# Half of each Q cast moved to ScalarE, three of eight scalings instead of two on GpSimd, last stores split: strided attention on one Trainium2 core

## Chip, cores and metric

The kernel runs on one core of a Trainium2 chip. The metric is the device time of one execution in microseconds (us). Every run has a state; all runs used here for comparison are in the fast state, and where a run fell in the slow one the text says so. The profile's engines are PE (TensorE), DVE (VectorE), ACT (ScalarE), POOL (GpSimd) and SPq (the sequencer of SyncE, which issues all transfers).

## The reference

```python
batch, heads, seq, dim = 8, 12, 1024, 64        # Q, K, V float32; stride 64
attend_positions = np.arange(0, seq, stride)    # the same 16 keys for every query
for i in range(seq):
    scores = einsum('bhqd,bhkd->bhqk', Q[:, :, i:i+1], K[:, :, attend_positions]) / sqrt(dim)
    weights = softmax(scores)
    result[:, :, i] = einsum('bhqk,bhkd->bhqd', weights, V[:, :, attend_positions])
```

All of Q (25.2 MB) is read, the result (25.2 MB) is written, and of K and V only every 64th row is needed. There is little arithmetic for each byte.

## The kernel before

The 96 heads are worked in 24 groups of four. A group's 1 MB block of Q is loaded, cast to bf16 on GpSimd, transposed on VectorE, multiplied with keys placed block-wise (`scores`), put through exp on ScalarE, multiplied with values (`outputs`, in three parts of 3, 2 and 3 token blocks), and divided by the sums of the weights, which come out of the same matmul.

```python
    def cast(g):
        qb[g] = qb_pool.tile([P, 32 * D], BF16, name="qb", tag="qb")
        nc.gpsimd.tensor_copy(out=qb[g], in_=qn[g])
    # ...
    def outputs(g, c):            # c = 0, 1, 2: 3, 2, 3 token blocks
        # ... n matmuls into ps, reciprocal r on VectorE
        if n == 3:
            nc.vector.tensor_tensor(out=to, in0=o, in1=by, op=ALU.mult)
        else:
            nc.scalar.copy(to, o)
            nc.gpsimd.tensor_tensor(out=to, in0=to, in1=by, op=ALU.mult)
    # ...
    key_rows(0)
    cast(0)
    cast(1)
    keys(0, 0)                    # two copies on ScalarE, two on VectorE
    transpose(0)
    scores(0)
    # ...
    for g in range(NG):           # each engine runs its instructions in this order
        # ahead(g): transpose(g+2), scores(g+1), values(g+2), cast(g+3); outputs(g, 0..2)
        if g % 2 == 1:
            for a in range(2):
                store(g // 2, a)                      # 1 MB
                if g - 1 + a + QBUFS < NG:            # QBUFS = 10 blocks of Q in SBUF
                    load(g - 1 + a + QBUFS)
```

All loads and stores go through one queue in the order in which they are written: K, block 0, V, blocks 1 to 9, then store, load, store, load for each pair of groups, and stores alone once all 24 blocks are loaded.

The softmax here doesn't subtract the row's maximum and nothing guards it: scores larger than these inputs give would overflow.

## Time and profile before

| What | Value |
|---|---|
| time, three runs | 129.98, 130.06, 130.66 us |
| span of the profiled run | 128.2 us |
| VectorE, GpSimd, TensorE, ScalarE busy | 75, 70, 54, 45% |
| transfer queue busy | 96.1% |

These groups of instructions (busy us in all, mean ns of one, idle time before them) are the ones that the change touches:

```profile
L199 POOL CAST qb<-qn 128x2048 bf16<-128x2048 f32 x24 | 45.3, 1889 | 3.9 <-DMA qn<-in_Q_dram 3.9
L249 DVE TENSOR_TENSOR out_sb<-o_ps,rec 128x768 f32<-128x768 f32 x48 | 46.0, 958 | 1.7
L252 POOL TENSOR_TENSOR out_sb<-out_sb,rec 128x512 f32<-128x512 f32 x24 | 25.0, 1042 | 23.2 <-ACT out_sb L251 23.2
L251 ACT COPY out_sb<-o_ps 128x512 f32<-128x512 f32 x24 | 14.1, 586 | 23.7 <-DVE rec L247 16.6 <-issue 5.5 <-POOL qb L199 1.6
```

The number before the comma is the busy time of the whole group: 46.0 us of VectorE goes into scalings, 45.3 us of GpSimd into casts, while ScalarE copies only 14.1 us. That is the imbalance that the change goes for.

### The profile page before, as it was taken

What the parts mean: (1) busy time and instruction counts of PE and PEld (TensorE: products, weight loads), DVE (VectorE), ACT (ScalarE), POOL (GpSimd) and SP (SyncE); (2) the same over time, 40 slices, a digit from 0 to 9 for tenths busy, and PEclk for the clock granted to TensorE, in tenths of its full rate; (3) what the DMA queues carried; (4) which work ended last, traced back from release to release, by engine and by line L of the source; (5) the groups of instructions that cost most, each with busy time, mean ns of one, the idle gap of its engine ahead of it and who ended that gap; (6) DMA issues with size and microseconds to landing.
All of it is one profiled execution on the core that took longest, in us unless ns stands there. A gap on an engine that the chain in (4) does not pass through costs nothing.

```text
span 128.2 us, 1125 instructions
## 1 busy us (share of the span) xinstructions
PE 69.1 (54%) x292; PEld 30.9 (24%) x292; DVE 95.6 (75%) x167; ACT 57.7 (45%) x96; POOL 90.2 (70%) x89
## 2 busy tenths in 40 slices
PE   0004267886763796348674664696436973465100
PEld 0001022342321343114331332333212431132000
DVE  6947557677988778898789888888889788987300
ACT  4110603638592448785264644535364255462100
POOL 8952489966888576897969888897889878533300
PEclk9999999999999559996579998559995589997555
DMA  2999989999998999999989999999999999989593
GB/s 64 363 325 465 470 358 470 409 419 389 430 417 368 476 394 430 440 384 432 488 363 440 440 419 435 424 404 470 419 404 435 419 424 424 424 353 440 251 430 164
DMA packets 6373, 51.18 MB, mean 399 GB/s; under 512 B 3872, under 2 KB 3872, under 8 KB 3872
## 3 DMA queue, kind: packets, MB, share of 16 engines
q1 hardware_dynamic: 6368, 51.12, 96.1%
q8 instruction: 2, 0.03, 0.1%
q14 instruction: 3, 0.02, 0.0%
HBM read 25.95 MB, written 25.17 MB: 399 GB/s over the span
## 4 chain that ended last, share of the span: by engine, by line
DVE 54%; PE 17%; issue 9%; DMA 8%; POOL 4%; SPq 1%; ACT 0%; POOLq 0%
DVE out_sb L249 32%; DVE qt L203 14%; PE o_ps L239 13%; DMA qn<-in_Q_dram 8%; DVE rec L247 7%; PE sc L210 4%; POOL out_sb L252 2%; POOL qb L199 1%; POOL v L191 1%; DVE v_rep L184 1%; SPq L35 1%; ACT out_sb L251 0%; SPq L100 0%; DVE k_r L159 0%; SPq L98 0%
## 5 line engine op out<-in xcount | busy, mean ns | idle before, releaser
L239 PE MATMUL o_ps<-v,w 128*128 128x260 bf16 x192 | 41.0, 340 | 34.0 <-DVE out_sb L249 32.5
L221 ACT ACTIVATE w<-sc 64x512 bf16<-64x512 f32 x48 | 35.5, 739 | 31.7 <-PE sc L210 31.0
L199 POOL CAST qb<-qn 128x2048 bf16<-128x2048 f32 x24 | 45.3, 1889 | 3.9 <-DMA qn<-in_Q_dram 3.9
L249 DVE TENSOR_TENSOR out_sb<-o_ps,rec 128x768 f32<-128x768 f32 x48 | 46.0, 958 | 1.7
L210 PE MATMUL sc<-qt,k_t 128*128 128x512 bf16 x96 | 34.7, 497 | 13.6 <-DVE qt L203 12.1
L252 POOL TENSOR_TENSOR out_sb<-out_sb,rec 128x512 f32<-128x512 f32 x24 | 25.0, 1042 | 23.2 <-ACT out_sb L251 23.2
L239 PEld LDWEIGHTS <-w 128*128 128x128 bf16 x192 | 19.2, 116 | 62.3 <-DVE out_sb L249 46.2
L203 DVE STREAM_TRANSPOSE qt<-qb 128x1024 int32<-128x1024 int32 x24 | 29.6, 1232 | 5.2 <-POOL qb L199 5.2
L247 DVE RECIPROCAL rec<-o_ps 128x12 f32<-128x12 f32 (+1 forms) x72 | 15.3, 213 | 15.9 <-PE o_ps L239 15.9
L251 ACT COPY out_sb<-o_ps 128x512 f32<-128x512 f32 x24 | 14.1, 586 | 23.7 <-DVE rec L247 16.6
L191 POOL TENSOR_TENSOR v<-mask,v_rep 128x256 bf16<-128x256 bf16 x24 | 16.0, 668 | 2.3 <-DVE v_rep L184 2.3
L210 PEld LDWEIGHTS <-k_t 128*128 128x128 bf16 x96 | 11.1, 116 | 24.9 <-issue 12.0
L169 ACT COPY k_t<-k_r 32x128 bf16<-32x128 bf16 x20 | 5.9, 295 | 1.7 <-DVE k_r L159 1.5
L129 POOL MEMSET k_t<- 128x4608 bf16 x1 | 3.9, 3935 | 0.0
L180 PE MATMUL vp<-v_bf,perm_v 128*128 128x384 bf16 x4 | 1.5, 413 | 2.4 <-DVE v_rep L184 2.4
L158 ACT CAST k_bf<-k_raw 128x256 bf16<-128x256 f32 x3 | 1.2, 405 | 3.5 <-DMA k_raw<-in_K_dram 3.4
L139 DVE TENSOR_SCALAR s_sel<-col,slot_f 128x4 bf16<-128x4 int16 x1 | 2.5, 2547 | 0.1
L184 DVE CAST v_rep<-vp 128x384 bf16<-128x384 f32 x4 | 2.1, 544 | 0.6 <-PE vp L180 0.6
L123 DVE MEMSET k_t<- 128x1152 uint32 x1 | 1.0, 1018 | 1.0 <-PEq L321 1.0
L158 ACT ACT_TABLE_LOAD x1 | 1.3, 1283 | 0.7 <-PEq L321 0.7
L127 DVE MEMSET w<- 128x512 uint32 x3 | 1.5, 485 | 0.2
L118 POOL COPY perm_v<-identity 128x32 bf16<-128x32 bf16 x8 | 1.2, 209 | 0.0
(16 smaller groups left out, 4.8 us busy)
## 6 DMA issues: line engine op xcount, KB each, us to landing
qn<-in_Q_dram SPq DMA_DIRECT2D x24, 1024.0 KB, 13.6
out_dram<-out_sb SPq DMA_DIRECT2D x24, 1024.0 KB, 11.2
k_raw<-in_K_dram SPq DMA_DIRECT2D x1, 384.0 KB, 4.7
v_raw<-in_V_dram SPq DMA_DIRECT2D x1, 384.0 KB, 7.8
```

The lines of the kernel that those rows point to most:

```text
L129: nc.gpsimd.memset(k_t[:, 8:NG], 0.0)
L169: op(k_t[dst : dst + 32, 8 * m + c : 8 * m + 8 : 2, :, col : col + NK], k_r[src : src + 32, 4 * m : 4 * m + 4].rearrange("p n (a k f) -> p ...
L191: nc.gpsimd.tensor_tensor(out=vb[g][:, 0 : 4 * D].rearrange("p (s d) -> p s d", s=4), in0=mask, in1=v_rep[:, g // 2, g % 2].unsqueeze(1).t ...
L199: nc.gpsimd.tensor_copy(out=qb[g], in_=qn[g])
L203: nc.vector.transpose(qt[g].bitcast(I32), qb[g].bitcast(I32))
L210: nc.tensor.matmul(sc, lhsT=k_t[:, g, f, NK * (1 - e) : NK * (1 - e) + P], rhs=_ap_with(q, [q.ap[0], [D, 8], [16 * D, 2], [2, 32]], extra_ ...
L221: nc.scalar.activation(out=_ap_with(wa, [wa.ap[0], [P, 8], [4, 32], [2, 2]], extra_offset=a), in_=sc[64 * a : 64 * a + 64].rearrange("p (t ...
L239: nc.tensor.matmul(ps[:, i, 0 : 4 * D + 4], lhsT=wt[g][:, i0 + i], rhs=vb[g], start=True, stop=True,)
L247: nc.vector.reciprocal(r, ps[:, 0:n, 4 * D : 4 * D + 4])
L249: nc.vector.tensor_tensor(out=to, in0=o, in1=by, op=ALU.mult)
L251: nc.scalar.copy(to, o)
L252: nc.gpsimd.tensor_tensor(out=to, in0=to, in1=by, op=ALU.mult)
```

## The change

ScalarE takes half of every cast. GpSimd scales three token blocks of eight instead of two (with ScalarE copying them out of PSUM first), VectorE five instead of six. The last two groups are stored each as soon as it is done.

```diff
     def cast(g):
         qb[g] = qb_pool.tile([P, 32 * D], BF16, name="qb", tag="qb")
-        nc.gpsimd.tensor_copy(out=qb[g], in_=qn[g])
+        half = 16 * D
+        nc.gpsimd.tensor_copy(out=qb[g][:, 0:half], in_=qn[g][:, 0:half])
+        nc.scalar.copy(qb[g][:, half:], qn[g][:, half:])
...
-        if n == 3:
+        if c < 2:
             nc.vector.tensor_tensor(out=to, in0=o, in1=by, op=ALU.mult)
...
-    def store(n, a):
-        o = out_2[n][a : P : 2]
+    def store(g, groups, a):
+        o = out_sb[g][a : P : 2]
...
-        if g % 2 == 1:
+        if g >= NG - 2:
+            for a in range(2):
+                store(g, 1, a)
+        elif g % 2 == 1:
             for a in range(2):
-                store(g // 2, a)
+                store(g - 1, 2, a)
                 if g - 1 + a + QBUFS < NG:
                     load(g - 1 + a + QBUFS)
```

More of the change, by code (lines that the diff above doesn't have):

```diff
@@ L259, in store @@
             _ap_with(
-                out, [[16 * D, 64], [2 * SD, 4], [1, 16 * D]],
-                2 * n * HG * SD + a * SD,
+                out, [[16 * D, 64], [2 * SD, 2 * groups], [1, 16 * D]],
+                g * HG * SD + a * SD,
             ),
-            _ap_with(o, [o.ap[0], [1, 1], [1, 64 * D]]),
+            _ap_with(o, [o.ap[0], [1, 1], [1, 32 * groups * D]]),
         )
```

## The prediction

> **What bounds the kernel now.** I began with the page's parts 1 and 2. No engine is full (VectorE 75%, GpSimd 70%, TensorE 54%), but the row of the DMA engines stands at 8 or 9 tenths from the second slice to the last few:
>
> ```profile
> DMA  2999989999998999999989999999999999989593
> ...
> q1 hardware_dynamic: 6368, 51.12, 96.1%
> ```
>
> Each digit is a fortieth of the span, 3.2 us. The queue that SyncE fills is busy 96.1% of 128.2 us, 123.2 us, for 51.12 MB. So the kernel is bound by transfers, and only the 5 us in which they stand still can be won. The second view, busy time in chosen stretches, shows where those are (the last two columns are the share of the DMA engines and GB/s; a share can pass 1 where packets overlap):
>
> ```profile
> 2.00:30.00 28.00, 13.02 (x39) 5.25 (x39) 19.15 (x37) 8.96 (x17) 20.69 (x19) 1.00 1.02 400
> ...
> 30.00:114.00 84.00, 53.24 (x240) 24.65 (x240) 70.56 (x121) 45.12 (x77) 65.96 (x58) 0.84 1.00 423
> 114.00:115.00 1.00, 0.40 (x2) 0.11 (x2) 0.89 (x2) 0.98 (x2) 0.02 (x1) 1.00 0.47 197
> 115.00:120.00 5.00, 2.46 (x11) 0.84 (x11) 3.60 (x9) 1.40 (x3) 1.97 (x2) 0.69 1.01 426
> 120.00:121.00 1.00, 0.00 (x0) 0.00 (x0) 0.41 (x1) 0.00 (x0) 0.11 (x1) 0.50 0.09 33
> 121.00:122.00 1.00, 0.00 (x0) 0.00 (x0) 0.00 (x0) 0.00 (x0) 0.00 (x0) 0.50 0.62 262
> 122.00:125.00 3.00, 0.00 (x0) 0.00 (x0) 0.00 (x0) 0.00 (x0) 0.00 (x0) 0.50 1.04 437
> 125.00:127.00 2.00, 0.00 (x0) 0.00 (x0) 0.00 (x0) 0.00 (x0) 0.00 (x0) 0.50 0.62 262
> ```
>
> From 2 to 114 us there is no hole. Then come three: 0.53 us before the second-last pair of groups is stored, 0.91 + 0.38 = 1.29 us before the last pair, and about 0.8 us at the very end, where some transfers end before others. The chain of waits (54% VectorE, 8% DMA) must be read with this in mind: it follows the last store back through compute, and that compute mattered only after 114 us.
>
> The start comes third, because compute must offer the first store before the first loads run out. Until 30 us the queue moved 374 GB/s x 30.0 us = 11.22 MB; the ten first blocks of Q (10 x 1.049 MB) with K and V (2 x 0.393 MB) are 11.27 MB. So the loads end at about 30.1 us. The timeline has the first store there only just in time:
>
> ```profile
> 7.35 0.60 ACT L169 COPY k_t<-k_r 32x128 bf16<-32x128 bf16 x2 [1.50 <-DVE k_r L159]
> 8.12 1.89 POOL L199 CAST qb<-qn 128x2048 bf16<-128x2048 f32 x1 [1.58 <-DMA qn<-in_Q_dram]
> 11.34 1.86 PE L210 MATMUL sc<-qt,k_t 128*128 128x512 bf16 x4 [11.34 <-DVE qt L203]
> 12.30 1.89 POOL L199 CAST qb<-qn 128x2048 bf16<-128x2048 f32 x1 [2.29 <-DMA qn<-in_Q_dram]
> 28.16 0.64 SPq L35 DMA_DIRECT2D out_dram<-out_sb  x1
> ```
>
> Data of a store moves about 0.9 us after its issue starts (estimate from the last pair: issued 120.47, and 262 of 437 GB/s in 121 to 122 us puts the start near 121.4). Issued at 28.16, the first store is ready at 29.1, one microsecond before the loads run dry.
>
> [...]
>
> **The change part by part.**
>
> *Work for each group of four heads.* VectorE drops one 768-element scaling (0.958 us) and takes one of 512[...]: busy 3.79 (0.64 reciprocals, 1.92 scalings, 1.23 transposition) becomes 3.5 us. GpSimd's cast of 2048 elements, 1.89, is halved to about 0.97; its scaling grows from 512 elements (1.04) to 768, about 1.45 by the slope between its 256-element (0.67) and 512-element products; values stay 0.67: 3.6 becomes 3.1. ScalarE has two exponentials (1.48), a copy grown from 0.59 to about 0.80, and a new half cast[...]: 2.07 becomes 3.3. The load is evened out, and nothing exceeds the old 3.8.
>
> *Pace of compute.* With the full TensorE clock a group takes 4.09 us now (scaling to scaling, 104.86 to 108.95), and VectorE is nearly full in it. Afterwards the loop is VectorE's 3.5 or a two-group loop through ScalarE copy, GpSimd scaling, values, cast and transposition, about 3.7. At the half clock the loop scaling, three matmuls (0.83), four score matmuls (1.9), first output matmuls, reciprocal takes 4.5 now (98.53 to 103.04) and contains nothing that changes. I take 3.95 instead of 4.2 as the mean. But both are under the DMA's need of 2.10 MB / 423 GB/s = 4.96 us per group, so between 30 and 114 us this is worth nothing for the end. It only makes the queue longer.
>
> *The tail.* With a queue that never empties, and with the last two groups stored when each is done (group 22 some 3 us earlier, only 1.05 MB left behind the last scaling), the two holes of 0.53 and 1.29 us go: **-1.8 us**. The uneven end of 0.8 us stays. The last scaling's own route gets longer (copy 0.80, GpSimd 1.45, against 0.96 on VectorE, about +1.3 us), but transfers queued in front cover it.
>
> *The start.* Here the order of instructions matters. ScalarE's half of cast(1) is written before the key copies keys(0,0), which the first scores need. ScalarE runs in order, so those copies (at 7.35 now) wait for Q block 1, which GpSimd receives at 12.30. Half cast to 13.3, two key copies to 13.9, scores(0) 13.9 instead of 11.34, first exponentials 15.8 to 17.4, second value matmul[...] to 17.9. So outputs(0) begin at 17.9 instead of 16.72: +1.2. Then group 0's last scaling is on GpSimd behind a ScalarE copy: copy 21.1 to 21.9, scaling to 23.4, values(2) to 24.1, half cast(3) to 25.1; transpose(3), which VectorE holds in front of group 1's reciprocals, starts at 25.1 instead of 23.14. First reciprocal of group 1 at 26.4 instead of 24.70; from there 4.65 us (two scalings, matmuls, copy, GpSimd scaling) instead of 3.46 to the store. The first store comes at about 31.1 instead of 28.16. Its data then starts at 32.0, the loads ended at 30.1: a hole of **+1.9 us** which no later work gives back, as the queue is full from there on. I followed the next stores the same way (40, 49, 58 us, against 36.93, 47.22, 55.59 now): each arrives before the queue is empty, if sometimes by only a microsecond.
>
> *Sum.* 130.06 - 1.8 + 1.9 = 130.2. The start is an addition of a dozen small terms of which I tended to take the long side, so I put the prediction at 129.9.
>
> **Rivals.** (a) The start isn't delayed as far as the loads' end: if the store comes before 29.2, only the tail counts, 130.06 - 1.8 = 128.3. For it: GpSimd's and ScalarE's halves run side by side, 0.9 us sooner per cast. Against it: the order of cast(1) and the keys is in the code, and the copy plus GpSimd scaling is longer by 1.3 us. (b) Compute is the bound, and relieving VectorE saves 24 x 0.25 = 6 us: 124. The chain of waits speaks for it, the full DMA row from 2 to 114 us against it; the floor of transfers, 51.12 MB at 423 GB/s = 120.9 us plus start, uneven end and close, leaves no room below about 128. (c) ScalarE becomes the bound: with keys (1.2 us) its groups 2, 3, 6, 7 need 4.5 us; if each semaphore wait costs a little more, stores 2 to 4 come late, more holes open early, and the time goes to 131.5 to 132.5. Its idle waits for scores (31.0 us now) say that it has room on average, but its position between PSUM banks and exponentials says that a late copy delays the next group's exponentials.
>
> **Range and chances.** The best case with no early hole is 128.3, the case with a hole of 3 us is 131.3; 128.4 to 131.4 should hold it 8 times in 10. Faster by over 2% needs under 127.46, below the floor of transfers: 0.05. Slower by over 2% needs over 132.66, an early loss of over 4.4 us: 0.05. Within 2%: 0.90.
>
> **What would show it.** Right: the key copies on ScalarE start near 13.3, the first store near 31, DMA rates fall in 30 to 32 us, no hole at 114 or 120, GpSimd casts near 1.0 us, VectorE's 512-element scaling 0.69, all compute done by about 121 while the queue is still long. Wrong: a first store before 29.2 (then 128.3), a hole between 40 and 60 us (rival c), or a queue still empty before the last store, which would mean that the pace of compute had become slower than 4.96 us per group.

## The result, and the profile after

The changed kernel took 131.88 us (median of four runs, 131.69 to 132.59); the kernel before, in the same rounds and the runs that came first, 130.28 us (129.98 to 130.66). Ratios here are the mean time of one kernel's fast runs over the mean of the other's fast runs of the same rounds, so they differ a little from the ratio of the medians. The ratio is 1.013, with an interval of 1.008 to 1.018: slower, though by less than 2%. The measured time lies 0.5 us above the predicted range.

The page of the changed kernel answers the first view of the prediction:

```profile
DMA  3999989997979999999999999999999999999991
...
q1 hardware_dynamic: 6528, 51.12, 96.0%
```

The queue is as busy as before, 96.0%, now of 130.1 us. The end of the row is full, as predicted; the 7s in slices 10 and 12 (from 29 and 36 us) are new. (A share counts a packet whole in the slice in which it starts. By the records of single packets only the first 7 is a standstill; in slice 12 the engines are busy with packets that started before it. A share over 1 can have two reasons: from 5 to 30 us of the kernel before up to 24 packets are on record at once, and the share is 1.02 even with packets cut at the window's edges; from 122 to 125 us, 1.04 becomes 1.01 in this way.) The groups of instructions, by form:

```profile
L201 ACT CAST qb<-qn 128x1024 bf16<-128x1024 f32 x24 | 25.1, 1045 | 7.6 <-DMA qn<-in_Q_dram 7.0
L200 POOL CAST qb<-qn 128x1024 bf16<-128x1024 f32 x24 | 24.9, 1037 | 5.2 <-DMA qn<-in_Q_dram 5.2
...
L254 POOL TENSOR_TENSOR out_sb<-out_sb,rec 128x768 f32<-128x768 f32 x24 | 35.3, 1471 | 29.4 <-ACT out_sb L253 29.4
L253 ACT COPY out_sb<-o_ps 128x768 f32<-128x768 f32 x24 | 19.2, 798 | 14.6 <-DVE rec L249 14.3
L251 DVE TENSOR_TENSOR out_sb<-o_ps,rec 128x512 f32<-128x512 f32 x24 | 16.6, 692 | 0.8
```

The engines do what the change meant them to do: casts on GpSimd fall from 45.3 to 24.9 us, scalings on VectorE from 46.0 to 39.6 (23.0 of 768-element ones and the 16.6 shown). None of this is where the time is. The start of the changed kernel, in its timeline:

```profile
7.71 1.04 ACT L201 CAST qb<-qn 128x1024 bf16<-128x1024 f32 x1 [2.22 <-DMA qn<-in_Q_dram]
...
11.87 1.04 ACT L201 CAST qb<-qn 128x1024 bf16<-128x1024 f32 x1 [3.11 <-DMA qn<-in_Q_dram]
...
12.82 0.60 ACT L169 COPY k_t<-k_r 32x128 bf16<-32x128 bf16 x2
...
13.47 1.89 PE L212 MATMUL sc<-qt,k_t 128*128 128x512 bf16 x4 [13.47 <-ACT k_t L169]
...
30.36 0.63 SPq L35 DMA_DIRECT2D out_dram<-out_sb  x1
```

ScalarE's half of block 1's cast waits for that block until 11.87 us, the key copies come behind it at 12.82, though their source `k_r` is ready at 7.31, and the first scores wait for them until 13.47 us, against 11.34 before. The first store is issued at 30.36 us, against 28.16. What that does to the queue is in the view of chosen stretches (last columns: granted TensorE clock, DMA share, GB/s), first of the changed kernel, then of the kernel before:

```profile
30.00:31.00 1.00, 0.47 (x3) 0.00 (x0) 0.97 (x3) 0.96 (x3) 1.00 (x3) 0.50 0.01 0
31.00:32.00 1.00, 0.28 (x2) 0.22 (x3) 0.96 (x3) 0.98 (x1) 0.94 (x1) 0.50 0.62 262
32.00:38.00 6.00, 5.11 (x18) 2.27 (x17) 4.64 (x9) 5.02 (x9) 3.08 (x3) 0.50 1.04 306
38.00:114.00 76.00, 46.64 (x230) 22.74 (x229) 61.51 (x116) 62.97 (x88) 55.95 (x54) 0.88 1.00 425
114.00:125.00 11.00, 1.69 (x8) 0.50 (x6) 2.23 (x5) 1.45 (x2) 2.94 (x2) 0.54 0.99 417
125.00:127.00 2.00, 0.00 (x0) 0.00 (x0) 0.00 (x0) 0.00 (x0) 0.00 (x0) 0.50 0.90 377
127.00:129.00 2.00, 0.00 (x0) 0.00 (x0) 0.00 (x0) 0.00 (x0) 0.00 (x0) 0.50 0.18 74
```

```profile
32.00:38.00 6.00, 4.34 (x20) 1.90 (x18) 5.45 (x9) 4.55 (x11) 4.99 (x6) 1.00 1.01 399
38.00:114.00 76.00, 47.49 (x216) 22.02 (x216) 63.96 (x111) 39.14 (x63) 60.08 (x52) 0.82 1.00 426
```

Three things are to be seen. First, the queue stands still at 30 us. The view makes it 0.99 + 0.38 = 1.4 us, but it counts each packet whole where it starts. By the records of single packets, those of load 9 end at 30.68 to 31.21 us (mean 30.89) and those of the first store begin at 31.65 to 31.79 (mean 31.70), so an engine stands still for 0.8 us on average. Second, and this was not foreseen, from 32 to 38 us the DMA engines are busy all the time (share 1.04) but move 306 GB/s instead of 399: the packets themselves take longer. By the records of single packets, 16 KB pieces of the first store go from 0.62 to 1.26 us and 32 KB pieces of the load behind it take about 1.75 instead of 1.22. Over all packets from 28 to 40 us this is 1.5 us more for each engine than before (1.9 against 0.4, in the table under x12). Third, the rate between 38 and 114 us is the same in both kernels, 425 and 426 GB/s: the new division of work is worth nothing there. And at the end the share falls over more than two microseconds, 0.90 and then 0.18: some engines end much later than others.

**A second look at the end.** The page counts 16 DMA engines, and the trace records the landing of a transfer in 16 steps (800 for the 50 transfers of the kernel before, 832 for the 52 of the changed one). I take one step for each engine. The trace has the time of each step but not the engine's name, so for every transfer one can work out when the median engine and when the last engine ended. This is my own working from the trace, times in us from the span's start:

```
                           before: median, last     changed: median, last
load 9 (last of the first)     31.1   32.1               31.3   31.7
first store, first half        33.8   34.5               35.4   35.5
load 10                        36.3   37.5               39.0   39.2
load 11                        41.4   42.4               44.0   44.7
store of groups 20 and 21     120.7  121.6              122.6  124.2
last store                    127.0  127.1              127.4  129.1
```

The engines fall out of step early and stay so: in the kernel before, the first and the last of the 16 are 1.0 to 1.4 us apart until 44 us and 2.0 to 2.2 us apart from 51 to 115 us; in the changed one 0.3 to 1.2 and then 2.1 to 2.3. In these two traces they come together by more than 0.3 us only where the queue has run empty: in the changed kernel from 0.57 us at load 9 to 0.26 at the first store, behind the hole at 30 us; in the kernel before they are 2.2 us apart at the landing of 116.65 us, 1.0 behind the hole at 114 us, and 0.2 behind the one at 120 to 122. Across the two holes the landings of the median engine are 3.1 and 3.9 us apart, those of the last engine 2.5 and 3.1, so it is the fast ones that waited. The changed kernel has no hole there, and its engines are 2.3 us apart at the last store.

So the holes at the end of the kernel before were mostly holes of the fast engines. The last steps of its last five transfers fall at 116.65, 119.12, 121.56, 124.70 and 127.14 us. They are 2.4 to 2.5 us apart, as in the stretch before, except for one of 3.14: the slowest engine did not notice the hole at 114 us at all, and lost 0.7 us, not 1.29, in the one at 120 to 122. Between load 11 and the store of groups 20 and 21, the last engine took 79.1 us before and 79.5 after; for what followed it took 5.6 us before (hole included) and 4.9 after. The whole difference of the last column, 2.0 us, is then 2.2 us up to load 11, 0.4 in the middle, and -0.6 at the end (from unrounded times).

### The profile page after: what moved, and what is told of

It reads as the page before. It is cut to its first block, busy times and chain, and to the rows that moved or that the text cites.

```text
span 130.1 us, 1201 instructions
## 1 busy us (share of the span) xinstructions
PE 65.9 (51%) x292; PEld 30.6 (24%) x292; DVE 88.8 (68%) x167; ACT 86.3 (66%) x120; POOL 80.1 (62%) x89
## 3 DMA queue, kind: packets, MB, share of 16 engines
q1 hardware_dynamic: 6528, 51.12, 96.0%
## 4 chain that ended last, share of the span: by engine, by line
DMA 35%; POOL 23%; issue 17%; DVE 5%; ACT 4%; PE 4%; SPq 1%; POOLq 1%; DVEq 0%; ACTq 0%
DMA qn<-in_Q_dram 35%; POOL out_sb L254 9%; POOL qb L200 8%; POOL v L191 5%; DVE out_sb L251 3%; PE sc L212 3%; ACT qb L201 2%; DVE qt L205 1%; POOLq L340 1%; ACT out_sb L253 1%; PE o_ps L241 1%; DVE rec L249 1%; ACT k_t L169 1%; ACT w L223 1%; SPq L35 1%
## 5 line engine op out<-in xcount | busy, mean ns | idle before, releaser
L241 PE MATMUL o_ps<-v,w 128*128 128x260 bf16 x192 | 39.0, 325 | 36.0 <-DVE out_sb L251 31.8
L254 POOL TENSOR_TENSOR out_sb<-out_sb,rec 128x768 f32<-128x768 f32 x24 | 35.3, 1471 | 29.4 <-ACT out_sb L253 29.4
L251 DVE TENSOR_TENSOR out_sb<-o_ps,rec 128x768 f32<-128x768 f32 (+1 forms) x48 | 39.6, 824 | 1.9 <-DVE rec L249 0.3
L212 PE MATMUL sc<-qt,k_t 128*128 128x512 bf16 x96 | 33.2, 481 | 14.0 <-ACT k_t L169 13.5
L201 ACT CAST qb<-qn 128x1024 bf16<-128x1024 f32 x24 | 25.1, 1045 | 7.6 <-DMA qn<-in_Q_dram 7.0
L253 ACT COPY out_sb<-o_ps 128x768 f32<-128x768 f32 x24 | 19.2, 798 | 14.6 <-DVE rec L249 14.3
L200 POOL CAST qb<-qn 128x1024 bf16<-128x1024 f32 x24 | 24.9, 1037 | 5.2 <-DMA qn<-in_Q_dram 5.2
L212 PEld LDWEIGHTS <-k_t 128*128 128x128 bf16 x96 | 10.9, 114 | 24.9 <-ACT k_t L169 13.5
L159 DVE STREAM_TRANSPOSE k_r<-k_bf 128x128 int32<-128x128 int32 x3 | 0.9, 308 | 2.3 <-ACT k_bf L158 2.3
```

The costliest lines, as they stand in the source:

```text
L200: nc.gpsimd.tensor_copy(out=qb[g][:, 0:half], in_=qn[g][:, 0:half])
L201: nc.scalar.copy(qb[g][:, half:], qn[g][:, half:])
L212: nc.tensor.matmul(sc, lhsT=k_t[:, g, f, NK * (1 - e) : NK * (1 - e) + P], rhs=_ap_with(q, [q.ap[0], [D, 8], [16 * D, 2], [2, 32]], extra_ ...
L241: nc.tensor.matmul(ps[:, i, 0 : 4 * D + 4], lhsT=wt[g][:, i0 + i], rhs=vb[g], start=True, stop=True,)
```

## The experiments

My theory after this reading was: (1) the hole before the first store costs its own length, (2) packets behind it are slow, and (3) the end is set by the slowest DMA engine, so filling the holes at the end pays only 0.6 us. The rival was that ScalarE's and GpSimd's new work slows the pace of compute. All kernels gave correct results. The numbers:

| Kernel | median us (lowest to highest) | ratio to before, interval |
|---|---|---|
| changed | 131.88 (131.69 to 132.59) | 1.013, 1.008 to 1.018 |
| x1 stores alone | 129.36 (129.22 to 129.47) | 0.993, 0.988 to 0.998 |
| x2 casts alone, its two fast runs of four | 131.68 (130.85 and 132.51) | 1.011, 1.000 to 1.021 |
| x3 copies and scalings alone | 132.33 (131.61 to 132.55) | 1.015, 1.009 to 1.020 |
| x4 changed, first groups as before | 129.89 (129.48 to 130.28) | 0.997, 0.992 to 1.002 |
| x5 changed, last stores as a pair | 131.71 (131.35 to 132.19) | 1.009, 1.002 to 1.017 |
| x6 changed, keys in front of cast(1) | 130.36 (130.01 to 130.45) | 0.999, 0.993 to 1.005 |
| x7 before, first store made late | 134.48 (133.38 to 135.15) | 1.030, 1.022 to 1.039 |
| x8 changed, loads two places ahead | 129.68 (129.45 to 129.79) | 0.994, 0.988 to 1.000 |
| x9 = x8 and extra loads on 8 engines | 132.33 (131.66 to 132.63) | 1.014, 1.007 to 1.020 |
| x10 changed, 8 engines kept busy | 133.70 (133.52 to 133.90) | 1.025, 1.018 to 1.032 |
| x11 before, stores alone, loads ahead | 129.36 (129.17 to 129.66) | 0.992, 0.987 to 0.997 |
| x12 changed, first two stores together | 131.50 (131.20 to 131.85) | 1.011, 1.003 to 1.019 |

The medians are of four runs each (x2: two, x11: six). The kernel before had medians of 130.08 to 130.29 us beside them, between 129.05 and 131.44 in its fast runs (one of its runs, beside x12, was slow). The batches ran at different times and on different chips, so differences between batches of a few tenths of a us are not to be read.

**x1: the single stores alone.** The kernel before with only the hunks of `store` and of its calls:

```diff
-        if g % 2 == 1:
+        if g >= NG - 2:
+            for a in range(2):
+                store(g, 1, a)
+        elif g % 2 == 1:
```

> Theory (the queue is the bound; the change lost time because the queue ran empty before the first store, its first packets afterwards were slow, and its engines ended unevenly): the stores alone leave the start as before, so the first store at 28.2 us, no hole there, 30 to 40 us at about 410 GB/s or more. At the end the hole of 1.3 us before the last pair goes, the uneven end may grow by up to 1 us: 128.8 to 130.1, best guess 129.3. Rival (the pace of compute, with more waits on ScalarE and GpSimd, is what costs): the stores touch no engine, so the same gain at the end, but no statement on unevenness: 128.7.

It took 129.36 us, 0.9 us less than the 130.25 beside it, and the start was as before (first store at 27.65 us, 433 GB/s from 32 to 38 us). The split of the stores is the good part of the change. The gain is about half of the 1.8 us that the prediction had booked, and near the 0.6 us of the last engine's column.

**x2 and x3: the casts alone, the copies and scalings alone.** x2 is the kernel before with the first of these two hunks, x3 with the second:

```diff
-        nc.gpsimd.tensor_copy(out=qb[g], in_=qn[g])
+        half = 16 * D
+        nc.gpsimd.tensor_copy(out=qb[g][:, 0:half], in_=qn[g][:, 0:half])
+        nc.scalar.copy(qb[g][:, half:], qn[g][:, half:])
...
-        if n == 3:
+        if c < 2:
```

> Theory: the split cast alone delays the first scores (ScalarE's key copies after block 1) to about 13.5 us, but shortens GpSimd's casts; the scaling stays on VectorE for six of eight blocks, so the first store at 28 to 29.3 us, hole at most 0.3 us: 129.8 to 130.6. Rival (ScalarE's longer queue is what costs): ScalarE has 3.1 us per group instead of 2.1, so most of the 1.8 us of loss should show here: 131.5 or more.

> Theory: the copy and scaling of three blocks on ScalarE and GpSimd, with GpSimd's whole casts, put 4.0 us per group on GpSimd and lengthen the route of group 0 and 1: first store at 30 to 31.5 us, a hole of 1 to 2 us at 30 us, slow packets after it (under 350 GB/s in 32 to 38 us); 131.5 to 133.5. Rival (ScalarE): ScalarE has only 2.3 us per group here, so near 130.

x2 is inconclusive: its profile and one more run of four fell in the slow state, and its two fast runs are 130.85 and 132.51 us, both above what the theory expected (129.8 to 130.6). In its profile the first store is at 28.56 us. x3 did what the theory said: first store at 30.09 us, no transfer from 30 to 31 us, 303 GB/s from 32 to 38 us, and 132.33 us, although ScalarE has little more to do in it than before.

**x4: the changed kernel with the first groups as before.**

```diff
     def cast(g):
+        if g < 4:
+            nc.gpsimd.tensor_copy(out=qb[g], in_=qn[g])
+            return
...
-        if c < 2:
+        if c < 2 if g >= 2 else n == 3:
```

> The changed kernel, but blocks 0 to 3 cast whole on GpSimd and groups 0 and 1 scaled as before. Theory: first store at 28.2 to 28.5 us, no hole, no slow stage after it (over 400 GB/s in 30 to 40 us), no hole at 114 and 120 us, uneven end as in the changed kernel (about 1.5 us): 128.3 to 129.5, best guess 128.9, faster than both kernels. Rival (steady pace or ScalarE bound): 20 of 24 groups are as in the changed kernel, so 131 to 132.

129.89 us: the first store at 28.14 us, 396 GB/s from 32 to 38 us, and 2.0 us less than the changed kernel, while the steady pace is the changed one for 20 of 24 groups. So the loss lies in the first groups, and the rival falls. The time is 0.5 us above x1 and 0.4 above my range, and the landings say why: the median engine ended its last store at 124.8 us, the last engine 2.25 us later.

**x5: the last two groups as a pair again.** The changed kernel with `store` and its calls as in the kernel before:

```diff
-        if g >= NG - 2:
-            for a in range(2):
-                store(g, 1, a)
-        elif g % 2 == 1:
+        if g % 2 == 1:
             for a in range(2):
-                store(g - 1, 2, a)
+                store(g // 2, a)
```

> The changed kernel with the last two groups stored as a pair again. Theory (the end is set by the slowest of the 16 DMA engines, whose queue is never empty at the end of the changed kernel): nothing to gain or lose, 131.5 to 132.3, ratio to the kernel before about 1.012. Rival (with the pair back, 2.1 MB wait behind the last scaling): 1 us or more slower, 132.9 and above.

131.71 us, the same as with single stores. In the changed kernel the queue is never empty at the end (share 0.99 from 114 to 125 us), so here it does not matter how the last stores are cut. They paid where the queue had run dry, as in x1 (0.9 us).

**x6: the key copies in front of block 1's cast.**

```diff
     cast(0)
-    cast(1)
     keys(0, 0)
+    cast(1)
```

> The changed kernel with ScalarE's key copies put in front of its half of block 1's cast. Theory: the first scores start near 10.2 us instead of 13.5, but the values wait (v_rep, near 16 us in both) holds outputs(0) to 16.5 to 17.1, so the first store moves only 0 to 0.6 us, to 29.8 to 30.4; the hole and the slow packets stay: 131.2 to 132. Rival (the prediction's step: the order of the keys is worth 1.2 us): first store at about 29.2, no hole, 129 to 130.

Here my expectation fell and the prediction's step held, though the first store came sooner, and the time was 0.4 us longer, than the rival said. In the timeline of this kernel:

```profile
8.30 0.60 ACT L169 COPY k_t<-k_r 32x128 bf16<-32x128 bf16 x2
...
9.87 1.87 PE L212 MATMUL sc<-qt,k_t 128*128 128x512 bf16 x4 [9.87 <-DVE qt L205]
...
28.45 0.63 SPq L35 DMA_DIRECT2D out_dram<-out_sb  x1
```

One line moved, and the first store comes 1.9 us earlier than in the changed kernel, nearly at its old place; the hole is gone and the time falls by 1.5 us to 130.36. I had thought that the values' wait would hold the first outputs back; they moved with the scores (they begin at 15.17 us, at 17.08 in the changed kernel and at 16.72 in the kernel before). The order alone does not explain the late store, however: x2 has it too, with its first store at 28.56 us (slow), and x3 has not, with its first store at 30.09. It is the late keys and the longer route over ScalarE and GpSimd together that make the store late. The slow stretch is not quite gone (363 GB/s from 32 to 38 us).

**x7: the kernel before, with a late first store.**

```diff
+        if g == 1:
+            for _ in range(2):
+                nc.vector.tensor_copy(out=out_sb[1], in_=out_sb[1])
         if g % 2 == 1:
```

> The kernel before, with two copies of a finished output tile onto itself on VectorE, so that its first store comes 2.3 to 2.7 us later (30.5 to 31) and the queue runs empty at 30 us, with nothing else of the change. Theory (a hole before the first store makes all 16 engines start together, and then the first packets are slow): hole of 1.3 to 1.9 us, the two landings after the first store spread over less than 0.4 us, 260 to 330 GB/s in 32 to 38 us as in the changed kernel, about 132.3 to 133.5. Rival (the slow packets come from ScalarE's or GpSimd's new work, not from the hole): hole, but over 380 GB/s in 32 to 38 us, and 131 to 132.

The copies took 2 us each, longer than I had reckoned, so the first store came at 31.70 us, later than intended, and the time is above my range. The stretches:

```profile
30.00:31.00 1.00, 0.00 (x0) 0.00 (x0) 1.00 (x1) 0.00 (x0) 0.54 (x1) 1.00 0.01 0
31.00:33.00 2.00, 0.00 (x0) 0.00 (x0) 1.97 (x4) 0.00 (x0) 0.00 (x0) 0.83 0.02 8
32.00:38.00 6.00, 3.62 (x12) 1.64 (x12) 5.08 (x9) 3.06 (x7) 3.31 (x3) 0.53 0.91 284
```

With nothing of the change in it, this kernel shows the same signature, a standstill and then 284 GB/s where the kernel before has 399 (its window from 32 us still holds 1 us of the standstill; from 33.5 to 39.5 us, where the engines are busy all the time, it is 306), and it loses 4.2 us. By the packet records the engines were idle 2.5 us more on average between 28 and 60 us, and their packets from 28 to 40 us took 1.5 us more than those of the kernel before; together 3.9. The execution that was profiled is the fastest of the four (133.38 us); its last landing came 3.0 us later than before, as its engines stood still for some 0.7 us less at the end. A late first store is enough to bring about both.

**x8: the loads two places ahead.**

```diff
+    load(QBUFS)
+    load(QBUFS + 1)
     for g in range(NG):
...
-                if g - 1 + a + QBUFS < NG:
-                    load(g - 1 + a + QBUFS)
+                if g + 1 + a + QBUFS < NG:
+                    load(g + 1 + a + QBUFS)
```

> The changed kernel with loads 10 and 11 issued before the first store (their buffers are free by 13 us), every later load two places ahead. Theory: the queue holds loads until about 35 us, so the first store at 30.4 us is no longer late: no hole, few slow packets (over 400 GB/s in 32 to 38 us), the slowest engine ends 2.5 us sooner than in the changed kernel: 128.9 to 129.9, faster than both kernels. Rival (the changed kernel is slow in its steady pace): no change, 131.5 or more.

The first store is as late as in the changed kernel, 30.36 us, but the queue has two more blocks to load, so nobody waits for it:

```profile
32.00:38.00 6.00, 5.08 (x22) 2.39 (x21) 4.54 (x9) 5.04 (x9) 3.08 (x3) 0.69 0.98 410
```

129.68 us, 2.2 us less than the changed kernel. That is the start's whole cost, hole and slow packets, in one number: where there was no hole to fill, the same loads ahead won nothing (x11 against x1, both 129.36 us).

**x9: more bytes on half of the engines.** x8, and in group 10 two useless loads whose outer size is 8.

```diff
... (x8's lines; the tile `spare`, which nothing reads)
+        if g == 10:
+            for i in range(2):
+                _copy(nc, spare[32 * i : 32 * i + 32], _ap_with(Q, [[128 * D, 8], [1, 128 * D]]))
```

> The changed kernel with loads two places ahead (the last run of the batch before, 129.68 us), and in the middle of it two useless loads of 262 KB whose outer size is 8, so that only 8 of the 16 DMA engines should carry them: 4 packets of 32 KB, up to 2.5 us for the 8 and nothing for the rest. Theory (the end is the end of the slowest engine, not of their average): either nothing (0 to 0.4 us, when the slowest is among the other 8, which end about 2.4 us behind the median) or the whole 2.5 us (2 to 2.5 us). Rival (the average counts, as the prediction reckoned): half, 1.2 us. The landings should show the split.

132.33 us, 2.65 us more than x8 (which ran in another batch). The trace has 32 packets more than the changed kernel's (6560 and 6528), 16 of data and 16 of completion: 8 completions for each useless load, where the other transfers have 16. That is two packets of data for each of 8 engines (not four, as I had written). At that place the distance from the first to the last landing grew from 2.1 to 4.3 us, and it did not shrink again until the end. The extra bytes are 1% of all; spread over 16 engines they would cost 1.2 us. They cost the full 2.5 us of an engine that carries them (two packets of 32 KB, of 1.24 us by the traces of the loads). In this run the end follows the slowest engine and not the average.

**x10 and x12: what makes the packets slow.** x10 puts the two useless loads behind load 9 of the changed kernel, so that 8 engines still work while the other 8 run dry. x12 keeps the hole but issues both halves of the first store before loads 10 and 11. First the edit of x10 (without the line that makes the tile `spare`), then that of x12, then the two expectations in the same order:

```diff
     for g in range(1, QBUFS):
         load(g)
+    for i in range(2):
+        _copy(nc, spare[32 * i : 32 * i + 32], _ap_with(Q, [[128 * D, 8], [1, 128 * D]]))
```

```diff
+            if g == 1:
+                store(0, 2, 0)
+                store(0, 2, 1)
             for a in range(2):
-                store(g - 1, 2, a)
+                if g > 1:
+                    store(g - 1, 2, a)
```

> The changed kernel with the same two useless loads behind load 9, so that at the first store 8 engines are still busy for 1 us or more while the other 8 have run dry: the engines then start 1 us or more apart. Theory (the slow packets come from all 16 starting together): spread of the first store's landing over 1 us, and the rate of 32 to 38 us up to 370 GB/s or more, excess packet time under 1 us per engine against 1.9. Rival (any hole before the first store makes them slow): under 330 GB/s and 1.6 to 2 us again. The time itself says little: 131 to 133.

> The changed kernel with its first two stores issued one behind the other and loads 10 and 11 after both, so that the hole at 30 us stays but no load stands between the two stores. Theory A (the packets after the hole are slow where the queue goes over from a store to a load with nothing else queued): the two stores run at full rate, and the slow packets move behind them or vanish; 31 to 36 us at 400 GB/s or more, 131 or less. Theory B (the first stores after a hole are slow as such): slow packets from about 33 us again, excess 1.5 to 2 us per engine, 131.5 to 132.3. I have no strong lean; the staggered run left this open.

The useless loads cost x10 1.8 us against the changed kernel, and its packets stayed slow: 295 GB/s from 32 to 38 us, an excess of 1.4 us for each engine: the rate is the rival's, the excess lies between the two expectations. The first store's first packets began at 31.18 to 31.88 us, 0.7 us apart and not the 1 us intended. The idea that all 16 engines must start together is not borne out, nor quite excluded. x12 says more:

```profile
32.00:34.00 2.00, 1.68 (x10) 0.68 (x8) 1.97 (x5) 1.46 (x4) 0.60 (x1) 1.00 1.03 426
...
36.00:38.00 2.00, 0.62 (x6) 0.40 (x5) 0.88 (x1) 1.95 (x3) 0.56 (x2) 1.00 1.22 360
```

The first store now runs at the full 426 GB/s right after the hole, and its packets take 0.62 us. The slow ones have moved to 35 to 38 us, the last packets of the second store and the first of load 10. So in this trace they are not a thing of the first writes; they come where the queue goes over from stores to the first load. The time, 131.50 us, hardly changed. My working of all traces, ordered by when the first store was issued (excess: packet time from 28 to 40 us above 0.616 us for 16 KB and 1.240 us for 32 KB, for each engine):

```
kernel    first store   hole   32-38 us    excess
x1           27.65      no     433 GB/s    0.1 us
x4           28.14      no     396         0.3
before       28.16      no     399         0.4
x6           28.45      no     363         0.8
x3           30.09      yes    303         1.9
x5           30.27      yes    306         1.8
changed      30.36      yes    306         1.9
x7           31.70      yes    284         1.9
x8           30.36, two loads still queued in front: 410, excess 0.1
```

Three traces are left out: x2 (28.56, slow: 0.9), x10 (29.82: 1.4) and x12 (30.20, with a hole: 1.2). The rate counts packets whole where they start and is coarse: x11, with an excess of 0.1 us, reads 397 GB/s, so the excess is the better measure. The less work stands in the queue in front of the first store, the slower are the packets behind it; a hole is not needed for it (x6). That is a relation over nine traces, of one profile each; its mechanism stays open.

**x11: no new split of work at all.** x1 with the loads of x8:

```diff
+    load(QBUFS)
+    load(QBUFS + 1)
     for g in range(NG):
...
-                if g - 1 + a + QBUFS < NG:
-                    load(g - 1 + a + QBUFS)
+                if g + 1 + a + QBUFS < NG:
+                    load(g + 1 + a + QBUFS)
```

> The kernel before with only the single stores at the end and the loads two places ahead. Theory (compute was never the bound before 114 us, so the new split of work is worth nothing once the queue is kept full): as good as the changed kernel with loads ahead, 129.0 to 129.8. Rival (the new split of work is worth something at the end): slower than 129.68 by 0.5 us or more.

129.36 us, the same as x1 and 0.3 us below x8. The new division of work on VectorE, ScalarE and GpSimd is worth nothing once the queue is kept full. x1 and x11 are the best kernels; both intervals lie below 1, so they beat the kernel before, by 0.7 to 0.8%, and the changed one, by 2.5 us.

## Why the prediction was wrong

**The bound: right.** Transfers bound both kernels, at 425 and 426 GB/s from 38 to 114 us. That they could not go faster was my assumption; no run tested it, and the highest rates that I read over 3 us or more are 437 GB/s in the kernel before (122 to 125 us) and 440 in x10 (116 to 120). Rival (b), compute as the bound, is out: x11 has the old pace and the same time as the best.

**The costs of the instructions: right.** VectorE's scaling 0.69 predicted, 0.692 measured; half cast on GpSimd 0.97 and 1.037; scaling of 768 there 1.45 (the slope that was named gives 1.41) and 1.471, which from 1.042 for 512 is 1.68 ns per element; copy on ScalarE 0.80 and 0.798; half cast on ScalarE 1.0 (12.30 to 13.3) and 1.045. The trace of the kernel before has no VectorE scaling of 512 elements, no ScalarE copy of 768 and no ScalarE cast of 1024; for these only the changed kernel's trace has the figures. With them VectorE's 3.5 and ScalarE's 3.3 us per group are 3.5 and 3.3 as measured.

**The pace: right, and worth nothing, as predicted.** From the fifth to the eighth pair's store, 64.08 to 89.12 us before and 65.47 to 88.20 us after, six groups took 4.17 and 3.79 us each, where I had said 4.2 and 3.95. (The stretches of the prediction at full and at half clock, 104.86 to 108.95 and 98.53 to 103.04 us, have a granted clock of 1.00 and 0.50 in the trace.)

**The start: right in its cause, off in its make-up.** The key copies start at 12.82 us (predicted 13.3), and the first store is issued at 30.36 (31.1). Of its delay of 2.2 us, the order of the keys was meant to be 1.2 us. That the second value matmul comes behind the first exponentials, as the prediction has it, is not shown: in the changed kernel it starts at 16.33 us, and they end at 16.87. And the first outputs begin only 0.36 us later than before (17.08 against 16.72): the late keys cost 1.9 us, as x6 shows, and block 0, with its cast halved and landed a little sooner in these executions, won 1.55 of them back. The longer route from there to the store is the rest, 13.28 us against 11.44: 1.84, where about 1.75 was predicted. The hole was 0.8 us and not 1.9. The loads ended at 30.9 us on average, where the prediction had 30.1, and data moved 1.3 us after the issue (31.65 - 30.36), where it had 0.9: both came from a view that counts packets whole where they start. The prediction then took the queue to be "full from there on" with normal packets; they were slow, which cost 1.5 us for each engine. On the last engine the start cost 2.2 us by load 11, against the +1.9 us booked, and x8 gives 2.2 us too. That the term is nearly right as a sum is luck: its hole was too long by 1.1 us, and the slow packets, which it did not know, made up for it.

**The tail: the step that failed.** "The two holes of 0.53 and 1.29 us go: -1.8 us. The uneven end of 0.8 us stays." I read the holes from a mean over 16 engines and took them to be time in which the transfers stood still. They were mostly time in which the fast engines waited for the slow ones, and across the two holes the spread of the 16 fell from 2.2 to 1.0 and 0.2 us, so the old end was even. On the last engine the hole of 0.53 us cost nothing and that of 1.29 us cost 0.7. Filling the holes is worth 0.6 us on the last engine in the changed kernel, and 0.9 us in x1. Nor was there an uneven end of 0.8 us that could stay: the 0.8 came from counting packets where they start. The 16 engines of the last store ended 0.2 us apart before, and end 2.3 us apart now. By x5 the single stores in the changed kernel are worth nothing at all.

**The sum again.** In terms of the last engine: 130.06 + 2.2 (start) + 0.4 (middle, unexplained and within what runs differ by) - 0.6 (end) = 132.1, measured 131.88. The tail term alone is 1.2 us of the 2.0 us by which 129.9 was missed.

**The rivals.** (a), no delay at the start, did not happen, but x4 and x8 are that case, and gave 129.7 to 129.9 instead of the 128.3 named for it, again for the tail. (c) named nearly the right time, 131.5 to 132.5, for the wrong reason: there was no hole between 40 and 60 us.

**Still open:** the mechanism of the slow packets, and what puts the DMA engines out of step. For the second there is only a coincidence: in every trace one packet of 16 KB of the instruction queue, lasting 0.9 to 1.1 us, falls between 47 and 54 us. Across it the spread of the landings grows by 0.8 to 1.3 us in seven of the 14 traces, the changed kernel's among them, but by 0.4 us in the kernel before and hardly at all in x7; and a second such packet, at 91 to 110 us, changes it by 0.2 us at most. No run tested it.

## What to carry to other kernels

In a kernel bound by its transfer queue, ask of each part of a change when it makes the first store ready and whether the queue still has work then; issuing two loads earlier, or moving one line so that an engine does not wait for data in front of something urgent, was worth more here (2.2 us in x8, 1.5 in x6) than 6 us less work on VectorE (nothing, x11 against x8). A hole in a mean over 16 DMA engines is not yet time to be won: look at the last engine of each transfer before booking it, and at single packets before measuring it, as a share that counts packets where they start can be off by half a us or more (1.4 against 0.8 us for the hole at 30 us). And splitting the last stores paid where the queue ran dry at the end (0.9 us in x1), not where it was full (x5).
